# A batched matmul bound by its transfers: stores of two pairs in one transfer, another engine leading the critical section, another one waiting at the end

## The chip, the core and the metric

The kernel runs on one core of a Trainium2 chip. A core has a matrix engine (TensorE, PE in the profile; its weight loads are PEld), VectorE (DVE), ScalarE (ACT), GpSimd (POOL) and SyncE (SP), and 16 transfer engines (DMA) that move data between the chip's main memory (HBM) and the on-chip SBUF. Transfers are issued from queues: here GpSimd's (a software queue, the only one used here that converts float32 to bfloat16 on the way) and SP's (a hardware queue). Each transfer is spread over all 16 transfer engines, and each engine works through a queue in order. A transfer is complete when all 16 have added 1 to its semaphore, 16 in all.

The metric is the device time of one execution in microseconds (us). Before the change it was 513.2 us, the median of three runs (512.89 to 513.69).

## The reference

```python
def setup_inputs():
    batch, m, k, n = 32, 512, 1024, 768
    return {
        "x": np.random.randn(batch, m, k).astype(np.float32),
        "weight": np.random.randn(batch, k, n).astype(np.float32),
    }

def reference(x, weight):
    return np.matmul(x, weight).astype(np.float32)
```

There are 32 independent products of a 512 x 1024 with a 1024 x 768 matrix. All inputs and outputs are float32 in HBM: 67 MB of x, 101 MB of weights, 50 MB of output.

## The kernel before

All of it is written out by hand, with hand-made semaphores, inside one critical section of the Tile framework (L374). That section has a leading engine, SP by default: at its start SP sets a semaphore on which the other engines wait, and at its end SP announces that it is done, every engine drains and answers, and SP collects the answers. A barrier over all engines, led by GpSimd, follows (L407). Lines of waits and transfers below are those of the profile.

**Tiling.** Weights of a batch are loaded as bfloat16 into one of four slots (`w`); batches 4 to 27 are loaded two at a time in one transfer (`load_w`, L100; the others at L104). x is loaded in pairs of batches, 2k+1 and 2k+2, into two slots (`load_x`, L117); batch 0 comes alone through SP (L375), batch 31 at L115. TensorE transposes x through PSUM (`transpose`, L169, eight groups for a pair of batches), VectorE spreads the transposed blocks into `both`, and TensorE multiplies (`multiply`, L150, four groups of 128 rows for a batch). The results of a group of rows leave PSUM through ScalarE (L281, L284) and VectorE (L295, L297).

**Outputs.** The results of two batches, 2a and 2a+1, fill one of four output slots, `outs[a % 4]`: rows of the first batch lie on 64 partitions, those of the second on the other 64, so that every partition holds 24 KB that are contiguous in HBM. `store` (L125) sends such a pair, 3 MB, in one transfer. Before ScalarE and VectorE write into a slot again, `slot_free` waits for the store of the pair four before. The last two batches, 30 and 31 (pair 15), go out as four half-batch stores of 768 KB from SP (`store_half`, L131), batch 30 from a slot of its own, `one`.

**Order of the work.** Each engine's program is a list in the order of the batches.
- GpSimd (`on_pool`) issues nearly all transfers. In the turn of an odd batch b it loads x of pair (b+3)/2, once that slot's transposes are done, then stores pair a = (b-5)/2, then loads the weights of batches b+3 and b+4, once batch b is multiplied. Pairs 0 to 10 are stored so. In the turn of batch 28, the last with loads behind it, it stores pairs 11, 12 and 13, one after the other.
- SP (`on_sp`) passes the arrival of weights on to TensorE, then issues the half of batch 30, pair 14 (3 MB), the second half of batch 30, and the halves of batch 31; all five count on `s_fin`, up to 80. It then sets `s_zero` and waits for `s_fin` (L363).
- TensorE (`pair_on_pe`) takes x, transposes a pair of batches, waits for weights (`take`, L173) and multiplies the two batches.
- GpSimd's last work, `clear_on_pool`, waits for its own stores (`s_st`) and for `s_zero`, then resets and clears all semaphores but `s_fin`.

Of the kernel before, what the change touches and what calls it, by code (L numbers as in the profile page):

```python
# [7 lines left out]
F32 = mybir.dt.float32  # L8
# [4 lines left out]
def kernel(  # L13
# [7 lines left out]
    B, M, K = x.shape  # L21
    _, _, N = weight.shape
    P = 128
    H = P // 2
    MT = M // P
# [3 lines left out]
    ROW = MT * N  # L29
    AHEAD = 3  # L30
    LATE = 4
    HELD = 4
    GROUPS = 2 * MT
    W_SLOTS, X_SLOTS, OUT_SLOTS = 4, 2, 4
# [3 lines left out]
    pe, dve, act, pool, sp = nc.tensor, nc.vector, nc.scalar, nc.gpsimd, nc.sync  # L38
# [3 lines left out]
    x_view = x.rearrange("b (mi mo) k -> b mi mo k", mi=P)  # L42
    pair_view = x[1:B - 1].rearrange("(p r) (mi mo) k -> p (r mi) mo k", r=2, mo=2 * MT)
    out_view = out.rearrange("b (mi mo) n -> b mi (mo n)", mi=P)
    two_view = out.rearrange("(p r) (i m) n -> p (r i) (m n)", r=2, m=2 * MT)

    def sbuf(name, shape, dtype):
        return nc.alloc_sbuf_tensor(name, shape, dtype).ap()
# [3 lines left out]
    ws = [all_ws[:, i] for i in range(W_SLOTS)]  # L52
    xs = [sbuf(f"x{i}", [P, 2 * MT, K], BF16) for i in range(X_SLOTS)]
    both = [sbuf(f"xT{i}", [P, 2, JT, 2, H, 2], BF16) for i in range(MT)]
    outs = [sbuf(f"out{i}", [P, 2 * ROW], F32) for i in range(OUT_SLOTS)]
    one = sbuf("one", [P, ROW], F32)
    x_first = outs[3][:, :MT * K].rearrange("p (mo k) -> p mo k", mo=MT)
    pts = [nc.alloc_psum_tensor(f"pt{i}", [P, JT, P], F32).ap() for i in range(2)]
# [6 lines left out]
    def sem(name):  # L65
        sems.append(nc.alloc_semaphore(name))
        return sems[-1]
# [7 lines left out]
    s_st = [sem(f"s_st{i}") for i in range(OUT_SLOTS)]  # L75
    s_fin = sem("s_fin")
# [9 lines left out]
    def out_done(b):  # L86
        return 2 * (b + 1)
# [4 lines left out]
    def together(b):  # L92
        return W_SLOTS <= b < B - W_SLOTS

    def load_w(b):
        if together(b):
            if b % 2 == 0:
                pool.wait_ge(s_mm, mm_done(b + 1 - W_SLOTS))
                slots = all_ws[:, b % W_SLOTS:b % W_SLOTS + 2].rearrange("p r ko n -> p r (ko n)")
                pool.dma_start(out=slots, in_=w_two_view[b // 2]).then_inc(s_w[b % W_SLOTS], 16)  # L100
            return
        if b >= W_SLOTS:
            pool.wait_ge(s_mm, mm_done(b - W_SLOTS))
        pool.dma_start(out=ws[b % W_SLOTS], in_=w_view[b]).then_inc(s_w[b % W_SLOTS], 16)  # L104

    def loads_of_w(b):

        return sum(not (together(i) and i % 2) for i in range(b % W_SLOTS, b + 1, W_SLOTS))

    def load_x(k):  # L110
        if k >= X_SLOTS:
            pool.wait_ge(s_pt, pt_done(k - X_SLOTS))
        slot = xs[k % X_SLOTS]
        if 2 * k + 1 == B - 1:
            pool.dma_start(out=slot[:, :MT], in_=x_view[B - 1]).then_inc(s_x[k % X_SLOTS], 16)  # L115
        else:
            pool.dma_start(out=slot, in_=pair_view[k]).then_inc(s_x[k % X_SLOTS], 16)  # L117

    def copied(eng, j):
        eng.wait_ge(s_ap, j + 1)  # L120
        eng.wait_ge(s_dp, j + 1)

    def store(eng, a, sem):
        copied(eng, out_done(2 * a + 1) - 1)
        eng.dma_start(out=two_view[a], in_=outs[a % OUT_SLOTS]).then_inc(sem, 16)  # L125

    def store_half(b, p):
        src = one if b == B - 2 else outs[(b // 2) % OUT_SLOTS]
        half = slice(p * N2, (p + 1) * N2)
        copied(sp, 2 * b + p)  # L130
        sp.dma_start(out=out_view[b, :, half], in_=src[:, half]).then_inc(s_fin, 16)  # L131
# [64 lines left out]
    def on_pe():  # L196
        pe.wait_ge(s_ident, 1)
        pe.wait_ge(s_first, 16)
        for g in range(GROUPS):
            if g > 1:  # L200
                pe.wait_ge(s_c, g - 1)
            transpose(0, g)
        pe.wait_ge(s_c, GROUPS).then_inc(s_c, -GROUPS)
        take(s_wr)
        for mt in range(MT):
            multiply(0, mt)
        with pe.Fori(0, LOOPS):
            for q in range(2):
                pair_on_pe(q, q)
            pe.wait_ge(s_c, 2 * GROUPS).then_inc(s_c, -2 * GROUPS)  # L210
            pe.wait_ge(s_a, 9).then_inc(s_a, -8)
            pe.wait_ge(s_d, 9).then_inc(s_d, -8)
        pair_on_pe(LOOPED, 0)
        b = B - 1
        take(s_xr)
        for g in range(MT):
            pe.wait_ge(s_c, GROUPS + max(g - 1, 0))
            transpose(b, g)
        take(s_wr)
        for mt in range(MT):  # L220
            j = 2 * b + mt // 2
            pe.wait_ge(s_c, GROUPS + mt + 1)
            pe.wait_ge(s_ap if mt % 2 else s_a, j - 1 if mt % 2 else 5 + mt // 2)
            pe.wait_ge(s_dp, j - 1)
            multiply(b, mt)
# [30 lines left out]

    def slot_free(eng, b):
        a = b // 2
        if a >= OUT_SLOTS and b % 2 == 0 and b < B - 2:
            eng.wait_ge(s_st[a % OUT_SLOTS], 16 * (a // OUT_SLOTS))  # L260
        if b == B - 1:
            eng.wait_ge(s_st[a % OUT_SLOTS], 16 * (a // OUT_SLOTS))

    def pieces(b, p, i):

# [9 lines left out]
    def out_on_act(b, p):  # L275
        j = 2 * b + p
        if p == 0:
            slot_free(act, b)
        act.wait_ge(s_mm, 2 * j + 1)
        for piece in pieces(b, p, 0):  # L280
            last = act.copy(*piece)  # L281
        last.then_inc(s_a, 1)
        act.wait_ge(s_mm, 2 * j + 2)
        act.copy(*pieces(b, p, 2)[0]).then_inc(s_ap, 1)  # L284
# [38 lines left out]

    def on_pool():
        load_w(0)
        pool.memset(ident, 0.0).then_inc(s_zero, 1)
        pool.wait_ge(s_zero, 1)
        pool.affine_select(
            out=ident,
            in_=ident,  # L330
            compare_op=mybir.AluOpType.not_equal,
            fill=1.0,
            base=0,
            pattern=[[-1, P]],
            channel_multiplier=1,
        ).then_inc(s_ident, 1)
        load_x(0)
        load_w(1)
        load_w(2)
        load_x(1)  # L340
        for b in range(B):
            if b % 2 and b + AHEAD + 1 < B:
                load_x((b + AHEAD) // 2)
            a = (b - 5) // 2
            if b % 2 and 0 <= a < B // 2 - 1 - HELD:
                store(pool, a, s_st[a % OUT_SLOTS])
            if b + AHEAD < B:
                load_w(b + AHEAD)
            if b == B - LATE:
                for a in range(B // 2 - 1 - HELD, B // 2 - 2):  # L350
                    store(pool, a, s_st[a % OUT_SLOTS])

    def on_sp():
        for b in range(B):
            if not (together(b) and b % 2):
                landed(sp, s_w[b % W_SLOTS], loads_of_w(b), s_wr, 1 + together(b))
        store_half(B - 2, 0)
        store(sp, B // 2 - 2, s_fin)
        store_half(B - 2, 1)
        store_half(B - 1, 0)  # L360
        store_half(B - 1, 1)
        sp.sem_inc(s_zero, 1)
        sp.wait_ge(s_fin, 80).then_inc(s_fin, -80)  # L363

    def clear_on_pool():

        for i, s in enumerate(s_st):
            pool.wait_ge(s, 16 * len(range(i, B // 2 - 2, OUT_SLOTS)))
        pool.wait_ge(s_zero, 2)
        used = range(sems[0].num, s_fin.num)  # L370
        pool.dma_reset(used)
        pool.sem_clear(used)

    with tc.tile_critical():  # L374
        sp.dma_start(x_first, x_view[0]).then_inc(s_first, 16)  # L375
        on_pool()
        on_pe()
        on_dve()
        on_act()
        on_sp()  # L380
        clear_on_pool()
# [30 lines left out]
```

## Time and profile before

| | |
|---|---|
| median of three runs | 513.2 us (512.89 to 513.69) |
| profiled execution, device time | 513.58 us |
| its span, first to last instruction | 511.8 us |
| mean granted TensorE clock | 0.946 |
| TensorE busy | 434.8 us (85%) |
| VectorE, ScalarE, GpSimd busy | 40%, 22%, 6% |
| transfers on GpSimd's queue | 14 stores of 3 MB, 12 weight loads of two batches, 8 of one, 16 loads of x |
| read and written in HBM | 167.77 MB and 50.33 MB, 426 GB/s over the span |

The profile is one execution. Its busy times don't add up to the span, since engines work side by side; the row of the transfer engines gives, for each of 40 slices of the span, the mean share of time in which they were busy, in tenths. The "GB/s" beside it counts bytes at the SBUF end: loads that turn float32 into bfloat16 count half of what they read. TensorE's clock is granted in steps: the profile lists stretches at full and at half clock.

### The profile page before, as it was taken

The numbers are of one execution on the slowest core, as the hardware profiler recorded it, in microseconds if no ns is written. First come the engines' busy times: TensorE is split into PE (matmuls) and PEld (weight loads), VectorE is DVE, ScalarE is ACT, GpSimd is POOL, SyncE is SP. The second block draws the span as 40 slices with busy tenths as digits, with TensorE's granted clock in tenths as the row PEclk, the third lists the DMA queues.
The fourth block names the chain that finished last, engine by engine and source line by source line (L and its number), as shares of the span: only waits on it lengthen the run. The fifth ranks groups of instructions, "written<-read, shape, count | busy, mean of one in ns | idle before, by whom it ended". The sixth has DMA issues, their size and how long they took to land. (4 is left out here: it accounts for less than half of the span.)

```text
span 511.8 us, 6037 instructions
## 1 busy us (share of the span) xinstructions
PE 434.8 (85%) x2528; PEld 278.5 (54%) x2576; DVE 207.0 (40%) x332; ACT 110.2 (22%) x189; POOL 29.8 (6%) x56
## 2 busy tenths in 40 slices
PE   0899975999998698987979989699897988999993
PEld 0666642666565364653646546365463644666561
DVE  0463540545445063451533525235252451545330
ACT  1013120132222112221212221122211222132210
POOL 3000000000101000010000100001000010010000
PEclk9999995999999799997989989799898997999998
DMA  8999999999999999999999999999999999999997
GB/s 255 212 216 218 224 208 224 208 230 327 220 331 220 242 312 223 332 221 254 297 224 335 219 267 283 217 340 215 277 273 220 335 219 298 256 217 249 428 428 309
DMA packets 9611, 135.40 MB, mean 265 GB/s; under 512 B 896, under 2 KB 896, under 8 KB 1408
## 3 DMA queue, kind: packets, MB, share of 16 engines
q0 software_dynamic: 8736, 126.88, 96.4%
q1 hardware_dynamic: 864, 8.39, 4.0%
q8 instruction: 5, 0.08, 0.1%
q14 instruction: 6, 0.05, 0.0%
HBM read 167.77 MB, written 50.33 MB: 426 GB/s over the span
## 5 line engine op out<-in xcount | busy, mean ns | idle before, releaser
L150 PE MATMUL pm<-w,xT 128*128 128x256 bf16 (+1 forms) x2000 | 351.0, 336 | 44.9 <-PEq L173 42.4
L150 PEld LDWEIGHTS pm<-w,xT 128*128 128x128 bf16 x2048 | 205.7, 101 | 188.1 <-issue 63.2
L295 DVE COPY out<-pm 64x512 f32<-64x512 f32 x120 | 82.5, 687 | 200.7 <-PE pm L150 199.9
L281 ACT COPY out<-pm 64x512 f32<-64x512 f32 (+1 forms) x122 | 70.7, 580 | 294.7 <-PE pm L150 294.0
L249 DVE COPY xT<-pt 128x1024 bf16<-128x1024 bf16 x112 | 72.2, 687 | 61.0 <-PE pt L169 61.0
L169 PE MATMUL pt<-ident,x 128*128 128x128 f32 x496 | 79.9, 302 | 10.5 <-DVE xT L249 9.5
L169 PEld LDWEIGHTS pt<-ident,x 128*128 128x128 f32 x496 | 69.2, 209 | 21.8 <-DVE xT L249 17.5
L284 ACT COPY out<-pm 64x512 f32<-64x512 f32 (+1 forms) x62 | 35.8, 578 | 89.7 <-PE pm L150 89.7
L297 DVE COPY out<-pm 64x512 f32<-64x512 f32 x60 | 41.2, 686 | 0.0
L117 POOL DMA_DIRECT2D x<-in_x_dram x15 | 8.3, 555 | 271.1 <-PE pt L169 270.9
L169 PE MATMUL pt<-ident,out 128*128 128x128 f32 x32 | 6.7, 360 | 12.7 <-DMA out<-in_x_dram 12.3
L100 POOL DMA_DIRECT2D w<-in_weight_dram x12 | 8.4, 703 | 112.8 <-PE pm L150 112.8
L169 PEld LDWEIGHTS pt<-ident,out 128*128 128x128 f32 x32 | 5.1, 206 | 14.1 <-issue 12.3
L232 DVE CAST xT<-pt 128x256 bf16<-128x256 f32 x16 | 6.2, 440 | 14.0 <-PE pt L169 13.8
L125 POOL DMA_DIRECT2D out_dram<-out x14 | 7.5, 537 | 0.7 <-DVE out L297 0.7
L104 POOL DMA_DIRECT2D w<-in_weight_dram x8 | 4.4, 556 | 19.2 <-PE pm L150 18.1
L247 DVE COPY xT<-pt 128x512 bf16<-128x512 bf16 x8 | 3.4, 420 | 4.1 <-PE pt L169 4.1
L292 DVE COPY out<-pm 128x512 f32<-128x512 f32 x2 | 1.4, 692 | 8.4 <-PE pm L150 8.4
L252 DVE COPY xT<-pt 128x1024 bf16<-128x1024 bf16 x4 | 2.6, 686 | 5.2 <-PE pt L169 5.2
L248 DVE COPY xT<-pt 128x512 bf16<-128x512 bf16 x8 | 3.3, 415 | 0.0
L292 DVE COPY one<-pm 128x512 f32<-128x512 f32 x2 | 1.4, 686 | 3.2 <-PE pm L150 3.2
L281 ACT COPY one<-pm 128x512 f32<-128x512 f32 x2 | 1.2, 585 | 4.0 <-PE pm L150 4.0
(9 smaller groups left out, 3.9 us busy)
## 6 DMA issues: line engine op xcount, KB each, us to landing
out_dram<-out POOLq DMA_DIRECT2D x14, 3072.0 KB, 29.7
w<-in_weight_dram POOLq DMA_DIRECT2D x12, 3072.0 KB, 34.1
x<-in_x_dram POOLq DMA_DIRECT2D x15, 2048.0 KB, 23.0
w<-in_weight_dram POOLq DMA_DIRECT2D x8, 1536.0 KB, 32.2
out_dram<-out SPq DMA_DIRECT2D x1, 3072.0 KB, 18.5
out<-in_x_dram SPq DMA_DIRECT2D x1, 2048.0 KB, 11.3
out_dram<-one SPq DMA_DIRECT2D x2, 768.0 KB, 12.4
out_dram<-out SPq DMA_DIRECT2D x2, 768.0 KB, 8.2
```

What stands on the lines that cost most here:

```text
L100: pool.dma_start(out=slots, in_=w_two_view[b // 2]).then_inc(s_w[b % W_SLOTS], 16)
L104: pool.dma_start(out=ws[b % W_SLOTS], in_=w_view[b]).then_inc(s_w[b % W_SLOTS], 16)
L117: pool.dma_start(out=slot, in_=pair_view[k]).then_inc(s_x[k % X_SLOTS], 16)
L125: eng.dma_start(out=two_view[a], in_=outs[a % OUT_SLOTS]).then_inc(sem, 16)
L150: last = pe.matmul(pm[bank][:, at:at + size], xT[:, ko // 2, :, ko % 2], w[:, ko, off:off + size], start=(ko == 0), stop=(ko == KT - 1),)
L169: last = pe.transpose(pts[g % 2][:, i, :], rows, ident)
L232: last = dve.tensor_copy(xT[:, 2 * (g % 2) + j].rearrange("p (h i) r -> p r h i", h=2), pt[:, 2 * j:2 * j + 2].rearrange("p r (i h) -> p r ...
L249: return dve.tensor_copy(tile[:, :, :, half].rearrange("p b j i r -> p j b i r"), pt)
L281: last = act.copy(*piece)
L284: act.copy(*pieces(b, p, 2)[0]).then_inc(s_ap, 1)
L295: last = dve.tensor_copy(*piece)
L297: dve.tensor_copy(*pieces(b, p, 2)[1]).then_inc(s_dp, 1)
```

## The change

It has three parts. First, the output slots become one tensor, so that two neighbouring slots can be sent in one transfer: GpSimd now stores pairs (0,1), (2,3), (4,5), (6,7) and (8,9) together, four batches and 6 MB each, in the turns of batches 5, 9, 13, 17 and 21, where pairs 0, 2, 4, 6 and 8 went; the turns of 7, 11, 15, 19 and 23 have no store. Pair 10 goes alone in the turn of batch 25, and in the turn of batch 28 pair 11 goes alone and pairs 12 and 13 together. A double store counts on the semaphore of its first slot, and `await_store` finds the count that a given pair's store brings. Second, the critical section is led by ScalarE, and its end leaves out GpSimd's drain. Third, GpSimd and not SP waits for the five last stores.

```diff
+    four_view = out.rearrange("(q s r) (i m) n -> q (r i) s (m n)", s=2, r=2, m=2 * MT)
...
-    outs = [sbuf(f"out{i}", [P, 2 * ROW], F32) for i in range(OUT_SLOTS)]
+    all_outs = sbuf("out", [P, OUT_SLOTS, 2 * ROW], F32)
+    outs = [all_outs[:, i] for i in range(OUT_SLOTS)]
...
-    def store(eng, a, sem):
-        copied(eng, out_done(2 * a + 1) - 1)
-        eng.dma_start(out=two_view[a], in_=outs[a % OUT_SLOTS]).then_inc(sem, 16)
+    STORES = [(a, 2) for a in range(0, B // 2 - 1 - HELD - 1, 2)]
+    STORES += [(B // 2 - 2 - HELD, 1), (B // 2 - 1 - HELD, 1), (B // 2 - HELD, 2)]
+
+    def store(eng, a, n, sem):
+        copied(eng, out_done(2 * (a + n - 1) + 1) - 1)
+        at = a % OUT_SLOTS
+        to, of = (four_view[a // 2], all_outs[:, at:at + 2]) if n == 2 else (two_view[a], outs[at])
+        eng.dma_start(out=to, in_=of).then_inc(sem, 16)
+
+    def store_on_pool(i):
+        a, n = STORES[i]
+        store(pool, a, n, s_st[a % OUT_SLOTS])
+
+    def await_store(eng, a):
+        first = next(i for i, n in STORES if i <= a < i + n)
+        done = sum(i % OUT_SLOTS == first % OUT_SLOTS for i, _ in STORES if i <= first)
+        eng.wait_ge(s_st[first % OUT_SLOTS], 16 * done)
...
     def slot_free(eng, b):
         a = b // 2
-        if a >= OUT_SLOTS and b % 2 == 0 and b < B - 2:
-            eng.wait_ge(s_st[a % OUT_SLOTS], 16 * (a // OUT_SLOTS))
-        if b == B - 1:
-            eng.wait_ge(s_st[a % OUT_SLOTS], 16 * (a // OUT_SLOTS))
+        if b == B - 1 or (a >= OUT_SLOTS and b % 2 == 0 and b < B - 2):
+            await_store(eng, a - OUT_SLOTS)
...
             a = (b - 5) // 2
-            if b % 2 and 0 <= a < B // 2 - 1 - HELD:
-                store(pool, a, s_st[a % OUT_SLOTS])
+            for i, (first, _) in enumerate(STORES[:-2]):
+                if b % 2 and a == first:
+                    store_on_pool(i)
...
             if b == B - LATE:
-                for a in range(B // 2 - 1 - HELD, B // 2 - 2):
-                    store(pool, a, s_st[a % OUT_SLOTS])
+                store_on_pool(-2)
+                store_on_pool(-1)
...
         sp.sem_inc(s_zero, 1)
-        sp.wait_ge(s_fin, 80).then_inc(s_fin, -80)
...
         pool.dma_reset(used)
         pool.sem_clear(used)
-
-    with tc.tile_critical():
+        pool.wait_ge(s_fin, 80).then_inc(s_fin, -80)
+
+    with tc.tile_critical(sync_engine=mybir.EngineType.Activation, no_gpsimd_drain=True):
```

More of the change, by code (lines that the diff above doesn't have):

```diff
@@ L357, in on_sp @@
         store_half(B - 2, 0)
-        store(sp, B // 2 - 2, s_fin)
+        store(sp, B // 2 - 2, 1, s_fin)
         store_half(B - 2, 1)
@@ L362, in on_sp @@
         sp.sem_inc(s_zero, 1)
-        sp.wait_ge(s_fin, 80).then_inc(s_fin, -80)
     def clear_on_pool():
         for i, s in enumerate(s_st):
-            pool.wait_ge(s, 16 * len(range(i, B // 2 - 2, OUT_SLOTS)))
+            done = sum(a % OUT_SLOTS == i for a, _ in STORES)
+            if done:
+                pool.wait_ge(s, 16 * done)
         pool.wait_ge(s_zero, 2)
```

## The prediction

> **What bounds the kernel now.** I read the page's summary first, then stretches of the end, then the two queues that issue transfers, and TensorE's waits last. From the page:
>
> ```profile
> PE 434.8 (85%) x2528; PEld 278.5 (54%) x2576; DVE 207.0 (40%) x332; ACT 110.2 (22%) x189; POOL 29.8 (6%) x56
> ...
> DMA  8999999999999999999999999999999999999997
> ...
> HBM read 167.77 MB, written 50.33 MB: 426 GB/s over the span
> ...
> PE 14%; DVE 1%; issue 0%
> ```
>
> The DMA row is 9 in all slices but the first and the last, while the chain of work covers only 15% of the span: what came before its start is a wait for a load. The 218.1 MB at 426 GB/s are the span: 16 transfer engines, never idle, set the time. TensorE (85% with its cold stretches) has some 5 us to spare for every two batches. So an edit counts for what it does to the transfer engines' first byte, to their work, to whether they run dry, and to what follows their last byte. The end, by stretches (us, PE, PEld, DVE, ACT and POOL busy, clock, DMA share, GB/s):
>
> ```profile
> 400.00:500.00 100.00, 93.59 (x558) 60.50 (x566) 42.95 (x74) 22.63 (x39) 5.33 (x10) 0.97 1.01 306
> ...
> 506.00:508.00 2.00, 0.00 (x0) 0.00 (x0) 0.00 (x0) 0.00 (x0) 0.00 (x0) 0.87 0.96 399
> 508.00:509.00 1.00, 0.00 (x0) 0.00 (x0) 0.00 (x0) 0.00 (x0) 0.00 (x0) 0.50 0.44 184
> 509.00:510.00 1.00, 0.00 (x0) 0.00 (x0) 0.00 (x0) 0.00 (x0) 0.00 (x0) 0.50 0.21 86
> 510.00:511.00 1.00, 0.00 (x0) 0.00 (x0) 0.00 (x0) 0.00 (x0) 0.00 (x0) 0.50 0.02 6
> ```
>
> The 16 engines don't end together. From 508 on a share of 0.44, then 0.21, works on: in the record of landings the first engine ends the last store at 508.20 and the last one at 510.64, 2.4 us later. That slowest engine is the kernel's bound, and it has work waiting to the end. The queues of SP and POOL (start, us, what):
>
> ```profile
> 503.72 0.33 SPq L131 DMA_DIRECT2D out_dram<-out  x1
> ...
> 347.99 0.54 POOL L125 DMA_DIRECT2D out_dram<-out  x1
> 357.83 0.70 POOL L100 DMA_DIRECT2D w<-in_weight_dram  x1 [9.31 <-PE pm L150]
> 378.37 0.56 POOL L117 DMA_DIRECT2D x<-in_x_dram  x1 [19.84 <-PE pt L169]
> 378.93 0.54 POOL L125 DMA_DIRECT2D out_dram<-out  x1
> 388.77 0.70 POOL L100 DMA_DIRECT2D w<-in_weight_dram  x1 [9.31 <-PE pm L150]
> 409.91 0.56 POOL L117 DMA_DIRECT2D x<-in_x_dram  x1 [20.43 <-PE pt L169]
> ```
>
> POOL issues in threes (x, store, weights of two batches), each set some 10 to 13 us before the weights already queued have landed (391.67 and 423.16 for those issued at 357.83 and 388.77). The last store goes out at 503.72. TensorE near the end:
>
> ```profile
> 392.00 11.95 PE L150 MATMUL pm<-w,xT 128*128 128x512 bf16 x63 [3.52 <-PEq L173]
> ...
> 409.66 10.35 PE L150 MATMUL pm<-w,xT 128*128 128x256 bf16 x62
> 423.48 0.80 PE L150 MATMUL pm<-w,xT 128*128 128x512 bf16 x2 [3.48 <-PEq L173]
> ```
>
> Each even batch waits for its weights (L173), and from batch 26 at 423.48 TensorE never waits for a load again: its end, 502.9, follows from that start.
>
> **1. Five pairs of stores become five transfers.** Before, pairs 0 to 9 leave POOL one at a time, ten transfers; after, five of 6 MB (with pairs 12 and 13 as a sixth), so 14 become 8. A double store goes out where its first pair did, so one set in two carries two stores and the next none. GpSimd waits no longer there: the same turn (batch 5, say) first waits for the transposes of batches 5 and 6, to load x, and the copies of batch 3, the last that the double store needs, were over before batch 4 was multiplied, more than 10 us earlier. The copies that use a slot again (slot_free) wait for a store that stands, in the same queue, ahead of the weights of their own batch, so that wait never ends last.
>
> What six transfers less save: the bytes are the same. Landings in unbroken queue traffic: a weight load of one batch 7.25 us (440.18 to 447.43 to 454.68), one of two batches 14.48 us (median of ten): two singles cost 0.02 us more than one double. That is the same edit on the other side. Upper bound: two stores of 7.30 us (mean of 11) against a double load of the same HBM bytes, 0.10 us. Lower bound: writes that alternate between places 3 MB apart could go slower; the paired weight load alternates over the same distance at no loss, so I allow 0.05 us for each of six the wrong way. Six times: -0.12 us near the paired load; I take -0.15, ends -0.6 and +0.3. (Title "DMA: Bandwidth & Descriptors", Anatomy of one DMA: the Trainium skill gives each transfer a fixed cost of about 2 us, mostly the receipt of its last write. By that, an estimate of 6 x 2 = 12 us would go, 501 us. The landings above, with 0.02 us, say that in a full queue it is hidden.)
>
> **2. Weights behind a double store land 7.3 us later, every second time.** TensorE then waits about 7.2 us for batches 8, 12, 16, 20 and 24 (before: 3.5 at 24) and little for 10 to 26. Two things hang on it.
>
> Does the queue run dry? At batch 20, say, weights land at 328.2 + 7.3 = 335.5, TensorE starts 0.3 later, the batch takes 13.2 (10.35, and 2.9 of cold clock as at 423.48), transposes 5.8: POOL issues x and the double store at 354.8. The weights queued by then land at 357.1 on the fastest engine and 359.9 on the slowest: 2.3 and 5.1 us left, against 3.6 and 5.0 at the smallest such place of before (x at 101.48, landings 105.1 to 106.4), which shows no gap. A fast engine that idles costs nothing until it has lost its 2.4 us lead. I take 0.
>
> Does TensorE's end move the last store? Weights of batch 24 at 391.67 + 7.3 = 399.0; start 399.3; batch 12.0 to 13.3 (rows 392.00 and 423.48, the latter 13.25 long), transposes 5.9, batch 25 10.4: batch 26 can start at 427.4 to 428.8, not at 423.5. Its weights, with the same bytes queued ahead of them as before, are there at 423.2, so it has no wait, and without one no cold start (-2.9). TensorE is then 1.0 to 2.4 us later to the end, and the last store goes out at up to 506.1. For the slowest engine that is enough: eight packets of 6144 B take it 1.9 us, it starts them at 508.4, and the store needs 1.0 us from issue to first byte (SP's first load: 0.95 to 1.96), so there are 508.4 - 504.7 = 3.7 us of slack. Cost 0; ends 0 and, see the rival, +1.5. (Title "TensorE: Matmul & The Clock Gate", Part 1: the Trainium skill says that an idle window of about 3.4 us puts the clock to half until one busy window has passed, so a wait twice as long costs no second penalty. The waits of 3.5 us here cost 1.6 and 2.9; by the page at most half of two windows, 3.4, an estimate, and batch 26 would start 0.5 us later than I have it, still within the slack.)
>
> **3. ScalarE leads the critical section.** At the start SP issues its event at 0.73 and its own first load at 0.95, behind it; that event (0.07 to its branch at 0.80, against 0.76 for ScalarE) moves to ScalarE, whose table load has 11 us of cover. SP's load comes 0.03 us sooner; GpSimd's path is as long. ScalarE's one event late in its copies has no reader waiting. -0.03, ends 0 and -0.07.
>
> **4. The end.** SP's last wait now:
>
> ```profile
> L363 SPq EVENT_SEMAPHORE  x1: 17/17/17, 510.7 to 510.7; - x1
> ...
> L374 SPq EVENT_SEMAPHORE  x3: 17/28/28, 510.7 to 510.9; - x3
> L374 SPq NOP  x2: 13/13/13, 0.7 to 511.0; - x2
> ...
> L407 POOLq EVENT_SEMAPHORE  x4: 17/17/17, 511.2 to 511.7; - x4
> ```
>
> From the last landing (510.64): SP wakes 510.66, tells all 510.72, engines drain 510.76 to 510.81, SP collects 510.88 and 510.95, event 511.02, drains to 511.13, GpSimd's first barrier 511.16, end 511.77. After: every engine but GpSimd has answered when TensorE ends; GpSimd wakes at 510.66, an event (about 0.08 between its own, 511.16 to 511.24), SP and ScalarE wake and drain (0.12), barrier at about 510.90. One trip out and back becomes one out: -0.25, ends 0 and -0.4. GpSimd's drain (0.05) ran beside the others'. Behind its new wait (on the five final stores) only the barrier is queued; its clearing of semaphores ran at 504.2 in both.
>
> Sum: -0.15 - 0.03 - 0.25 = -0.43 us. On the profiled execution: span 511.8 to 511.4, time 513.58 (span and 1.8 around it) to 513.15. That execution is 0.4 above the median of the runs, 513.2, from which I get **512.8 us**. A measurement here tells about 0.2%, 1.0 us: this is within it.
>
> **Rivals.**
> - *The last store comes too late (slower).* Batch 24 and batch 26 both run cold: then TensorE is 5.3 us late (7.3 - 3.5 + 1.5), 1.6 beyond the slack of 3.7, and with -0.43 the time is 514.4. For: every wait over 2.6 us in the trace brought half clock. Against: batch 26 has no wait left. It decides from 3.7 us of lateness; over 0.2% from 5.2. The same price falls due if the slowest engine waits for POOL in three of the five long turns by 0.5 us. Chance 0.10.
> - *More is saved (faster).* The six transfers save 0.10 each, the barrier 0.4, and the slowest engine loses 0.2 or more of its 2.4 us lag, which grew over the run (0.7 us at 25 us, 2.8 at 390): 513.2 - 0.6 - 0.4 - 0.2 = 512.0. For: lag is the slow engines' alone, and nothing says that it doesn't come with transfers. Against: it jumps at instruction fetches (0.8 at 30 us), which stay. Chance 0.22.
> - *The merge does nothing.* Transfers save 0, the end 0.25: 512.9, in the same class as the forecast.
>
> **How the numbers follow.** Forecast with the third rival 0.68, slower 0.10 (0.12 with what I don't see), faster 0.20. The likeliest case alone runs from 512.2 to 513.5 (sum of the ends and the 0.4 between runs). For 8 in 10 I go to the faster case, 511.9, and most of the way to the slower, 514.0.
>
> **What would show it.** Eight out_dram transfers on POOL's queue instead of 14, six of them of 6 MB; DMA at 9 throughout; waits at L173 alternating between about 7 and under 1 us; last matmul 1 to 2.4 us later, at 504 to 505.3, with the last landing unchanged at about 510.4; from there to the end 0.85 us instead of 1.1. I am wrong if the DMA share falls below 1 in mid-run, if all 16 engines end together after the last store's issue, or if the double stores take much else than 14.5 us to land.

## The result: slower by 0.27%, and where the time went

The changed kernel takes 514.35 us in the median of 14 executions (513.11 to 519.03), the kernel before 513.36 us (512.89 to 513.93) beside it on the same chip. The two medians are 0.99 us apart. The ratio on record is 1.0027, with an interval of 1.0014 to 1.0040, which leaves no change out; the time lies outside the predicted range of 511.9 to 514.0. The spread has changed too: the fastest five executions lie at 513.1 to 513.5, among those of before, while five of the 14 take 515 us or more, which the kernel before never did.

The profiled execution of the changed kernel took 514.30 us (span 512.5), that of before 513.58 (span 511.8). From the page of the changed kernel, its summary:

```profile
DMA  8999999999999999999999999999999999999997
...
HBM read 167.77 MB, written 50.33 MB: 426 GB/s over the span
...
L167 PE MATMUL pm<-w,xT 128*128 128x256 bf16 (+1 forms) x2048 | 349.6, 334 | 50.2 <-PEq L190 50.2
...
out_dram<-out POOLq DMA_DIRECT2D x6, 6144.0 KB, 29.5
```

The row of the transfer engines is as full as before: nothing here says that they ran dry. The waits for weights, L173 before and L190 now, have grown to 50.2 us: one of 1.1 us at the start and six of 7.4 to 8.6 us, in place of twelve of 42.4 us together. The six transfers of 6 MB are there.

The end, by stretches as before (us, PE, PEld, DVE, ACT and POOL busy, clock, DMA share, GB/s):

```profile
506.00:508.00 2.00, 0.00 (x0) 0.00 (x0) 0.00 (x0) 0.00 (x0) 0.00 (x0) 1.00 1.02 427
508.00:509.00 1.00, 0.00 (x0) 0.00 (x0) 0.00 (x0) 0.00 (x0) 0.00 (x0) 1.00 0.89 369
509.00:510.00 1.00, 0.00 (x0) 0.00 (x0) 0.00 (x0) 0.00 (x0) 0.00 (x0) 0.96 0.43 180
510.00:511.00 1.00, 0.00 (x0) 0.00 (x0) 0.00 (x0) 0.00 (x0) 0.00 (x0) 0.50 0.16 68
```

Compared with before, the decline begins one microsecond later: a share of 0.43 at 509 where it was 0.44 at 508. In the record of landings the first engine ends the last store at 509.14 (before 508.20) and the last one at 511.61 (before 510.64). The distance between them is the same, 2.47 and 2.44 us. So the first and the last engine are late by nearly the same, 0.94 and 0.97 us. They did not wait for the last store: it was issued at 505.77, and the share is still 1.02 from 506 to 508.

The time before that end holds the loss. Each packet of a kind has a usual duration in the trace; a packet of x, which writes 16 KB, takes 1.227 us. Summed over all packets that take over 0.05 us more than usual, the excess, divided by 16 engines, is 1.66 us before and 2.62 us after: 0.95 us more, which is the later end. The largest lot, 0.99 us, is in one load of x, the one that GpSimd issues at 291.44, in front of the double store of pairs 8 and 9. GpSimd's queue there, in the changed kernel (start, us, what):

```profile
291.44 0.57 POOL L119 DMA_DIRECT2D x<-in_x_dram  x1 [26.36 <-PE pt L186]
292.00 0.71 POOL L133 DMA_DIRECT2D out_dram<-out  x1
301.84 0.71 POOL L102 DMA_DIRECT2D w<-in_weight_dram  x1 [9.12 <-PE pm L167]
```

The weights queued ahead of that load landed at 294.14 on the first engine and 296.03 on the last. The first packet of x ran at 293.85, 2.41 us after its issue. The stretches over that load of x, which ends at about 306:

```profile
294.00:301.00 7.00, 7.00 (x45) 4.21 (x43) 1.98 (x3) 2.67 (x5) 0.00 (x0) 1.00 1.00 212
301.00:304.00 3.00, 3.00 (x20) 1.78 (x19) 1.98 (x3) 0.58 (x1) 0.71 (x1) 1.00 1.08 164
304.00:308.00 4.00, 4.00 (x27) 2.42 (x25) 1.14 (x2) 1.74 (x3) 0.00 (x0) 1.00 0.90 367
```

In the kernel before, the same load was issued at 283.34, and its first packet ran at nearly the same time, 293.75. The same stretches there:

```profile
294.00:301.00 7.00, 4.35 (x20) 2.34 (x21) 1.47 (x3) 0.28 (x2) 0.44 (x1) 0.76 1.03 220
301.00:304.00 3.00, 3.00 (x21) 1.73 (x19) 0.61 (x1) 1.52 (x3) 0.00 (x0) 1.00 1.03 257
304.00:308.00 4.00, 3.95 (x26) 2.44 (x26) 1.37 (x3) 1.16 (x2) 0.00 (x0) 1.00 0.97 408
```

In the changed kernel the share in the last column but one stays near 1, but the bytes in the last column fall from 212 to 164 GB/s from 301 to 304. The engines are busy with packets of x that take up to 2.1 us. This is a loss that the row of tenths cannot show. It sits in the last third of the load, some nine to thirteen microseconds after it was issued.

### The profile page after: what moved, and what is told of

Its sections match the earlier page's. It is cut to its first block, busy times and chain, and to the rows that moved or that the text cites. A ratio compares the mean times of both kernels' runs of the same rounds, so it can differ in the third digit from the quotient of the medians.

```text
span 512.5 us, 6075 instructions
## 1 busy us (share of the span) xinstructions
PE 431.7 (84%) x2576; PEld 277.6 (54%) x2576; DVE 206.9 (40%) x332; ACT 110.3 (22%) x189; POOL 27.7 (5%) x50
## 5 line engine op out<-in xcount | busy, mean ns | idle before, releaser
L167 PE MATMUL pm<-w,xT 128*128 128x256 bf16 (+1 forms) x2048 | 349.6, 334 | 50.2 <-PEq L190 50.2
L133 POOL DMA_DIRECT2D out_dram<-out x8 | 5.3, 668 | 1.3 <-DVE out L312 1.3
```

The source lines that it names most:

```text
L133: eng.dma_start(out=to, in_=of).then_inc(sem, 16)
L167: last = pe.matmul(pm[bank][:, at:at + size], xT[:, ko // 2, :, ko % 2], w[:, ko, off:off + size], start=(ko == 0), stop=(ko == KT - 1),)
```

## The experiments

I call the time from the issue of a load of x to its first packet its *lead*: how much work the queue still held. Loads are named by the pair they bring: x4 is issued in the turn of batch 5, x5 in that of batch 7, x6 in that of batch 9, and so on up to x14 in that of batch 25. In the changed kernel the even ones go out in the turns of a double store (x14 in that of a single one), with only the weights ahead of them.

The theories: first, that the double store itself costs time, by its shape; second, that the later order does, in that the queue is short when x and the store are issued; third, that the cost comes from addresses, when the rows of x and the bytes around them lie an even 32 KB apart; fourth, that the end is at fault. Later ones are told where they came up.

### The merge alone

Part one of the change, with SP leading and waiting as before:

```diff
         sp.sem_inc(s_zero, 1)
+        sp.wait_ge(s_fin, 80).then_inc(s_fin, -80)
...
-        pool.wait_ge(s_fin, 80).then_inc(s_fin, -80)
...
-    with tc.tile_critical(sync_engine=mybir.EngineType.Activation, no_gpsimd_drain=True):
+    with tc.tile_critical():
```

> The double stores alone, with SP leading and waiting as before. In the profile of the changed kernel every us lost against before lies in a few stretches in which the packets of an x load (16 KB written, 1.23 us each) take 1.4 to 2.1 us on all 16 engines: 0.96 us at 301 to 304, 0.28 at 428 to 430. Theory A (the double stores bring more such stretches): median 514.3 to 514.9, runs spread over 2 us or more, as with the whole change, plus the 0.27 us that the end's part saved. Rival B (the part with ScalarE and GpSimd at the ends makes the loss): 513.0 to 513.5, runs within 1 us.

Measured: 513.65 us (513.31 to 519.88, 12 runs) against 513.27, the median of the kernel before, run beside it; ratio 1.0033 (1.0007 to 1.0058). Four of the 12 are at 515 or above. The median lies between the two ranges that I had named, but the spread is that of theory A: the slowing and the scatter come with the merge.

### The ends alone

Parts two and three on the kernel before:

```diff
-        sp.wait_ge(s_fin, 80).then_inc(s_fin, -80)
...
+        pool.wait_ge(s_fin, 80).then_inc(s_fin, -80)
...
-    with tc.tile_critical():
+    with tc.tile_critical(sync_engine=mybir.EngineType.Activation, no_gpsimd_drain=True):
```

> ScalarE leading and GpSimd waiting alone, with single stores as before. Theory A: the last landing as before and 0.85 us instead of 1.13 from there to the end, so 0.3 us less than before, about 513.1, runs within 1 us. Rival B: 514 or more, runs spread over 2 us.

Measured: 513.18 us (512.63 to 514.13, 11 runs) against 513.27; ratio 0.9998 (0.9990 to 1.0007), no execution above 514.2. The ends cost nothing; what they save is too little for this measurement, and is read from the profiles below.

### Two single stores in the place of a double one

The kernel before, with two stores of 3 MB, one right behind the other, where the double store would go:

```diff
-            if b % 2 and 0 <= a < B // 2 - 1 - HELD:
-                store(pool, a, s_st[a % OUT_SLOTS])
+            if b % 2 and 0 <= a < B // 2 - 1 - HELD and a % 2 == 0:
+                for i in range(a, min(a + 2, B // 2 - 1 - HELD)):
+                    store(pool, i, s_st[i % OUT_SLOTS])
```

> As before, but two single stores go out in the turns in which the change sends a double one, and none in the turns between: the bytes stand in the queue in the order of the change, in 14 transfers instead of 8. Theory A1 (the order, or what it does to the time at which x loads and GpSimd's issues meet, is to blame): 514.3 to 515, spread over 2 us or more, weights of every second pair 7.3 us late. Rival A2 (the shape of the 6 MB transfer, two places 3 MB apart written in turn, is to blame): 513.2 to 513.6, within 1 us.

Measured: 513.72 us (513.42 to 519.31, 12 runs); ratio 1.0026 (1.0004 to 1.0047), with two executions at 518 and 519. Again the median falls between the two ranges and the spread decides: the slowing and the scatter come without any transfer of 6 MB: it is where the bytes stand in the queue, not the shape of the transfer. The first theory falls.

### Other addresses for x

The changed kernel, with the pair loads of x reading from the weights, 36 KB apart from partition to partition and not 32:

```diff
+    PITCH = 2 * MT * K + K
...
-            pool.dma_start(out=slot, in_=pair_view[k]).then_inc(s_x[k % X_SLOTS], 16)
+            pool.dma_start(out=slot, in_=pair_at(k)).then_inc(s_x[k % X_SLOTS], 16)
```

> The whole change, but the pair loads of x read other data: 32 KB for each partition as before, but out of the weights and 36 KB apart instead of 32 KB, so the products of batches 1 to 30 are of wrong numbers; sizes, order and counts of all transfers are the same. Theory C (the slow stretches come from x rows 32 KB apart, a power of two, when engines come to read in step): no x packet over 1.3 us, 512.4 to 512.8, runs within 1 us. Rival (the stretches have to do with the order of traffic or with GpSimd's issues, whatever the addresses): 514.3, spread over 2 us.

Measured: 513.30 us (513.13 to 514.71, 11 runs); ratio 1.0004 (0.9995 to 1.0013), in neither of the two ranges. The scatter was gone but for one execution, which spoke for addresses. But the leads of its profiled execution were 2.81 to 4.16 us, longer than those of the changed kernel (2.38 to 3.57), so that the two theories had not been told apart. The tenth run below does so.

### The double store ahead of x

The changed kernel, with the store issued in front of the load of x in each turn:

```diff
         for b in range(B):
-            if b % 2 and b + AHEAD + 1 < B:
-                load_x((b + AHEAD) // 2)
             a = (b - 5) // 2
...
+            if b % 2 and b + AHEAD + 1 < B:
+                load_x((b + AHEAD) // 2)
```

> The whole change, with the double store issued ahead of the x load in its turn instead of behind it. It waits only for copies that are done some 20 us before TensorE has finished the transposes that the x load waits for, so 14.5 us of stores lie in the queue when x is issued. Theory D (the late weights make GpSimd issue x 2.4 to 3.5 us before the first engine needs it, and in executions where TensorE is a little colder the queue runs dry): no execution over 514, median 512.4 to 512.8, issue of x to its first packet over 12 us everywhere. Rival O (two stores in a row, in whatever place, disturb the transfers): 513.5 to 514.5, with executions of 515 to 519 in 2 to 5 of 12.

Measured: 513.27 us (513.09 to 513.55, 11 runs) against 513.14; ratio 1.0002 (0.9993 to 1.0011). Of the load of x nothing is lost any more: every x has 7 us or more queued ahead of it, and no packet of x took longer than usual. The scatter is gone. But this is not the 512.4 to 512.8 that I had expected: the loss went, and a gain over before did not appear. In this order the store of pairs 8 and 9 does not wait for the transposes, so it goes out 24.9 us ahead of x:

```profile
266.37 0.72 POOL L133 DMA_DIRECT2D out_dram<-out  x1 [1.63 <-DVE out L312]
291.27 0.54 POOL L119 DMA_DIRECT2D x<-in_x_dram  x1 [24.19 <-PE pt L186]
```

It runs from 294 to 301 at full rate, but it was not issued at a short queue, so this run doesn't tell what a store would lose there:

```profile
294.00:301.00 7.00, 7.00 (x46) 4.22 (x44) 1.99 (x3) 2.50 (x5) 0.00 (x0) 1.00 1.01 427
```

### x made late without any change of stores

The kernel before, with GpSimd waiting for three of the four groups of the batch before it issues x and the store, from the turn of batch 9 on:

```diff
             if b % 2 and b + AHEAD + 1 < B:
+                if b >= 9:
+                    pool.wait_ge(s_mm, 4 * b + 3)
                 load_x((b + AHEAD) // 2)
```

> Before, with single stores in their old order, but from the turn of batch 9 on GpSimd also waits for three of the four groups of that turn's batch before it issues x and the store, 7.8 us later than now: from issue of x to its first packet 2 to 5 us instead of 9 to 13. Theory D: executions of 515 or more in several of 12, median 514 or more. Rival O (the order of the stores): like before, 513.2 to 513.4, within 1 us.

Measured: 521.77 us (519.77 to 522.50, 5 runs) against 513.14; ratio 1.0156 (1.0141 to 1.0172). In its profiled execution the leads of x alternate between 3.1 to 5.4 us and 1.25 to 1.48 us. Each of the first kind loses 0.08 us or less, each of the four short ones 1.80 to 2.08 us. All slow packets of that execution make 8.7 us, against 1.7 before; its span was 8.9 us longer than that of before (520.7 against 511.8). The rest is idle time at the short places, 0.7 us in the mean of the engines, and engines that end further apart. Single stores, doubles left out, ends as before: a short queue is enough for the loss. From the queue and the stretches of this run:

```profile
294.65 0.56 POOL L117 DMA_DIRECT2D x<-in_x_dram  x1 [31.22 <-PE pm L150]
```

```profile
301.00:304.00 3.00, 3.00 (x13) 1.50 (x12) 0.00 (x0) 0.08 (x1) 0.00 (x0) 0.56 1.08 208
304.00:308.00 4.00, 4.00 (x26) 2.44 (x25) 1.45 (x3) 1.66 (x3) 0.00 (x0) 1.00 0.94 160
```

x was issued three microseconds later than in the changed kernel, and the dip to 160 GB/s comes some three microseconds later too, at 304 to 308, again about ten microseconds after the issue.

### A shorter multiplication

The changed kernel, with six of the eight K parts multiplied, so that TensorE is done sooner and x is issued sooner:

```diff
-        for ko in range(KT):
+        for ko in range(KT - 2):
...
-                    stop=(ko == KT - 1),
+                    stop=(ko == KT - 3),
```

> The whole change, with the products over 6 of the 8 parts of K only (the last two left out of every batch). All transfers and their order are unchanged; TensorE needs about 2.6 us less for a batch, so GpSimd issues x and the double store 2.6 us earlier after the late weights: 5 to 6 us to the first packet instead of 2.4 to 3.5. Theory D: no execution over 514, median 512.4 to 512.9. Rival O: as the whole change, 514.3, spread to 519.

Measured: 512.70 us (512.48 to 513.12, 11 runs) against 513.14; ratio 0.9992 (0.9983 to 1.0001), an interval that just takes in no change. With double stores, x in front of them and the new ends all in place, and the lead longer (5.0 to 6.4 us at the double turns), the loss is gone. The lead is not all that differs: TensorE also does less, and the last store goes out at 487.91 and not at 505.77. The load issued at 291.44 in the changed kernel goes out at 287.75, and its stretches stay up:

```profile
287.75 0.57 POOL L119 DMA_DIRECT2D x<-in_x_dram  x1 [31.63 <-PE pt L186]
```

```profile
301.00:304.00 3.00, 3.00 (x20) 1.84 (x19) 1.69 (x3) 1.38 (x3) 0.00 (x0) 1.00 1.03 268
304.00:308.00 4.00, 3.51 (x24) 3.01 (x23) 2.58 (x4) 0.58 (x1) 0.00 (x0) 1.00 0.98 414
```

### Single stores ahead of x

The kernel before with the new ends, and each single store in front of its load of x:

```diff
         for b in range(B):
-            if b % 2 and b + AHEAD + 1 < B:
-                load_x((b + AHEAD) // 2)
...
+            if b % 2 and b + AHEAD + 1 < B:
+                load_x((b + AHEAD) // 2)
             if b + AHEAD < B:
...
```

> Before, with ScalarE leading and GpSimd waiting at the end as in the change, single stores in their turns, but each store issued ahead of the x load. Theory D: as the ends alone (513.18, 512.63 to 514.13 measured), the queue never short, and nothing more to gain: 512.8 to 513.2. Rival O2 (the small losses in x packets, some 0.4 us in every profile so far, come where a store follows an x load in the queue): 512.4 to 512.7, no x packet over 1.3 us beyond the first.

Measured: 515.45 us (514.85 to 515.77, 5 runs); ratio 1.0043 (1.0029 to 1.0057). Neither expectation foresaw this. It is another loss: no load of x is slow here (0.01 us at most), all slow packets together make 1.8 us, about what they make before (1.7). But a few engines fall behind the others. Of the weights that land around 330, twelve engines have brought theirs by 326.33 and the other four at 327.36, 329.21, 329.40 and 329.94. The landings of one transfer spread over 4.4 us there and 5.4 us at 440, against 2.6 to 2.8 before, and the last store ends at 512.76 on the slowest engine, 3.7 us after the median one. Around the end of the weights ahead of most stores, three to six packets took 0.1 to 0.9 us longer than usual. Why some engines pay for that order was not found.

### Doubles to pair 7, singles behind them

To take the better order where it helps and leave the end of the program as before: pairs 0 to 7 as double stores ahead of x, pairs 8 and 9 as singles behind it.

```diff
-    STORES = [(a, 2) for a in range(0, B // 2 - 1 - HELD - 1, 2)]
+    STORES = [(a, 2) for a in range(0, 8, 2)] + [(8, 1), (9, 1)]
...
+            a = (b - 5) // 2
+            for i, (first, n) in enumerate(STORES[:-2]):
+                if b % 2 and a == first and n == 2:
+                    store_on_pool(i)
             if b % 2 and b + AHEAD + 1 < B:
                 load_x((b + AHEAD) // 2)
...
+                if b % 2 and a == first and n == 1:
```

> A version that takes what the runs so far point to: double stores for pairs 0 to 7 only, each ahead of its x load; pairs 8, 9 and 10 singly, behind their x loads, as before; the ends as in the change. Queue never short (12 us or more from issue of x to its first packet in the double turns, 9 or more in the others), and TensorE's last wait for weights at batch 26 again, so its end at 503 and not at 504 to 505. Theory D: 512.7 to 513.0, no execution over 514, so a little under before. If the stores of the double turns cost by themselves: 513.3 or more.

Measured: 513.58 us (513.04 to 515.71, 12 runs); ratio 1.0008 (0.9997 to 1.0019). Three of the 12 stand above 514. In its profiled execution (514.61 us) all loads of x but one lose nothing; x12, at the border between the two orders, is issued at 354.83 with a lead of 1.89 us and loses 1.66 us. I had overlooked that border: the last double store leaves TensorE late by one turn more, and there x stood first again.

### Late x from other addresses

The late x of the sixth run, with the addresses of the fourth (both edits as above, on the kernel before).

> The kernel with the late x issue (521.8 us), with the pair loads of x reading weights 36 KB apart instead of x rows 32 KB apart, so the products of batches 1 to 30 are of wrong numbers. Theory D: the loss comes from the short queue alone, 520 to 523. Rival C (the addresses of x are what makes a short queue costly): 514 or less.

Measured: 520.94 us (520.56 and 521.32); ratio 1.0150 (1.0132 to 1.0168). Loads with leads of 1.30 to 1.48 us lose 1.50 to 2.01 us, as they did from x itself. The theory of addresses falls; the fourth run was fast for its leads.

### Two more executions of the changed kernel

The changed kernel itself, unedited, twice, to see the lead in executions of different length.

> The changed kernel again, for the profile of one of its slow executions (five of 14 were at 515 or more). Theory D: in an execution of 515 or more, one or more of the even x loads 6 to 14 has a first packet less than 2.3 us after its issue and loses 1 to 2 us over its packets; in one under 513.6 none does.

> As the look before: one more execution of the changed kernel. Theory D: its time stands above 512.7 by what the even x loads with short queues lose in it, within 0.5 us.

Measured: 520.55 and 514.62 us. The long one shows, at the same places as in the first profile, leads of 2.08, 1.29, 1.31 and 1.28 us at x8, x10, x12 and x14, and losses of 1.23, 1.70, 1.83 and 1.65, together 6.4 us; its span is 7.0 us longer than that of the kernel before. So the expectation for a long execution held. From its queue and stretches:

```profile
293.50 0.57 POOL L119 DMA_DIRECT2D x<-in_x_dram  x1 [27.26 <-PE pt L186]
```

```profile
294.00:301.00 7.00, 7.00 (x46) 4.26 (x45) 3.81 (x6) 1.74 (x3) 0.77 (x2) 1.00 1.01 204
301.00:304.00 3.00, 2.95 (x20) 1.73 (x19) 0.36 (x1) 1.52 (x3) 0.10 (x1) 1.00 1.03 197
304.00:308.00 4.00, 4.00 (x27) 2.44 (x26) 1.62 (x3) 1.38 (x3) 0.61 (x1) 1.00 0.93 213
```

At 304 to 308 the store should be running at 367 GB/s or more, and x is still at 213. The short one of the two has one lead below 2.8 us, 2.31 at x14, and loses 0.83 there. Its expectation failed: all its even loads lose 1.0 us, which gives 513.7 and not 514.62. Here one engine ended the last store at 511.93, 1.5 us after all others (510.46; in the first profile 511.61 after 511.45). So not every long time of the changed kernel is loss in x, and why that engine was late is open.

All loads of x with their first packet after 100 us and a lead under 6.5 us, in the profiled executions of all kernels here, before and after among them (us; a loss is the mean over 16 engines of what its packets took beyond the usual):

| lead from issue to first packet | loads | loss in each |
|---|---|---|
| 1.25 to 1.48 | 10 of a full pair of batches | 1.50 to 2.08 |
| 1.29 | 1 of a single batch | 0.31 |
| 1.89 and 2.08 | 2 | 1.66, 1.23 |
| 2.31 to 2.91 | 10 | 0.00 to 0.99, median 0.23 |
| 3.01 to 6.38 | 44 | 0.00 to 0.15 |

Not one lead is shorter than 1.25 us. Whether the queue still holds 3 us or 10 makes no difference (of the loads above 6.5 us, one lost 0.39 us and the others 0.10 at most); from 3 us down to 2 the loss grows to more than a microsecond. It is not the idle time of a queue that ran empty, which at leads of 2.4 us did not happen (at 1.3 us it comes on top, with 0.1 to 0.2 us). It is in packets that take longer: at the leads of 2.08 us and less, 0.1 to 0.6 us in the first half of the load and 1.1 to 1.7 in the second.

One rival to the lead alone is not tested. Each of the 22 loads of a full pair with a lead under 3 us had a store right behind it in the queue. With the store there and a lead of 3 us or more the loss was 0.15 us or less but for one load with 0.39, so the store alone is not the cause; whether a short lead without a store behind it would cost the same, no run shows. The one load that had weights behind it (1.29 us, a single batch) lost its 0.31 us in its first packets, and it was over 9 us after its issue.

Much of the scatter follows from this, in a way that I read from two executions and didn't test by an edit. A loss of 1 us delays all that stands behind it, the next long wait of TensorE ends later, the batch after the wait starts later by so much (at 404.38 in the long execution, 399.50 in the profiled one), and the next x is issued nearer to the end of its queue. A lead once below 2.1 us stays there: 2.08, 1.29, 1.31, 1.28.

### Is the rest the order at the border, or the late end?

The ninth run with its border mended: pair 8, too, is stored ahead of x.

```diff
-                if b % 2 and a == first and n == 2:
+                if b % 2 and a == first and (n == 2 or a == 8):
...
-                if b % 2 and a == first and n == 1:
+                if b % 2 and a == first and n == 1 and a != 8:
```

> The version with double stores of pairs 0 to 7 ahead of their x loads, mended where its queue fell short: pair 8, stored singly, also goes ahead of its x load; pairs 9 and 10 go behind theirs. Waits from issue of x to its first packet are then 8 us or more everywhere, so no execution over 514 by theory D. If what the store-first version (513.27) still misses of 512.7 is TensorE's late end, this one, whose weights for batch 26 come when they come before, stands at 512.7 to 512.9. If it is the slowest transfer engine, which falls back by 0.35 us where a double store follows weights, it stays at 513.1 to 513.4.

Measured: 513.09 us (512.80 to 513.54, 11 runs) against 513.08; ratio 0.9998 (0.9989 to 1.0007). With the border mended, no load of x from x4 on loses more than 0.05 us and the scatter is gone, but there is no gain.

And the fifth run with the last three batches (29 to 31) multiplied over six of eight K parts, so that TensorE ends sooner than before (the last store goes out at 497.10, before at 503.72):

```diff
-        for ko in range(KT):
+        parts = KT - 2 if b > B - 4 else KT
+        for ko in range(parts):
...
-                    stop=(ko == KT - 1),
+                    stop=(ko == parts - 1),
```

> The store-first version (513.27), with the products of batches 29, 30 and 31 over 6 of the 8 parts of K only, so TensorE ends about 7.5 us sooner and the last stores are issued well before the engines are free; all else is the same. Late end: 512.7 to 512.9. Slowest transfer engine: 513.1 to 513.3.

Measured: 513.10 us (512.87 to 513.44, 11 runs) against 513.08; ratio 0.9999 (0.9990 to 1.0008). The fifth run stood 0.13 above its own kernel before and this one 0.02, so that a late end can have cost the fifth some 0.1 us, less than either interval tells. What else keeps the fifth, the thirteenth and this one from the 0.4 us that the shorter multiplication shows was not settled. In their profiled executions the slowest engine is further behind, by 2.7 to 3.4 us in the median of the landings between 440 and 476 us, against 2.3 in the shorter multiplication and 2.4 with the ends alone; but it was 2.8 in the kernel before too, and 2.0 in the fourth run with its 513.30 us. Three executions of the changed kernel had 2.7, 2.7 and 3.5, so this is no account.

No version that does all of the work was faster than the kernel before by more than the measurement tells: the only one with a median lower by 0.4 us leaves a quarter of the multiplication out.

## Why the prediction was wrong, step by step

**The step that failed is in part 2, "Does the queue run dry?", with its price "I take 0".** Its working was near enough: I had 2.3 us left on the fastest engine at a long turn, counted to the landing of the weights ahead, and by that count the profiled execution had 2.70, 2.73 and 3.07 at three of them and 3.63 and 3.65 at two. (As leads, which end some 0.3 us sooner, these are 2.41, 2.38, 2.73, 3.29 and 3.34.) What failed is the price. I reasoned that a queue with 2.3 us left is not dry, that only a fast engine would idle, and that it had a lead of 2.4 us over the slowest one to lose. The runs show another loss: with less than about 3 us queued, packets of the load of x take longer, the slowest engine's among them (the load issued at 291.44 landed at 304.74 on the first and 307.14 on the last engine, the same load before at 303.79 and 306.35). In the profiled execution the three short leads cost 0.99, 0.39 and 0.22 us. In other executions leads of 2.1 us and below, about what my 2.3 us comes to as a lead, cost 1.2 to 2.1 us per full load.

I had compared with one place of before, "x at 101.48", that showed no gap. By its lead of 3.31 us (3.6 in my reckoning) it lies just on the harmless side. The row nearest to 2.3 was not near enough, and I did not bound the price from the other side, as I did for the transfers. The rival of the slower side named the right turns ("the slowest engine waits for POOL in three of the five long turns") but took the loss for idle time of 0.5 us, and gave it no chance of its own.

It also made my own sign useless. "I am wrong if the DMA share falls below 1 in mid-run" can't show packets that are busy for longer: the share was 1.08 while the bytes fell to 164 GB/s. The column of GB/s beside it, over a few microseconds, would have been the sign.

**Part 1, the merge: right as to its price, as far as it can be told.** A double store lands 14.58 and 14.59 us behind the transfer ahead of it (at 194.30 and 130.95), as the two singles did, 2 x 7.30. The Trainium skill's fixed cost of about 2 us for each transfer (title "DMA: Bandwidth & Descriptors", Anatomy of one DMA) would have given 12 us for six transfers, an estimate; no run here gained more than 0.44 us, so in a full queue it is hidden, as the landings of before said. With the lead made longer (the shorter multiplication), merge and ends together gave -0.44 us beside a forecast sum of -0.43. That kernel also leaves work out, and its interval takes in no change, so the agreement is no proof of the single terms. A slip that moves nothing: my upper bound of 0.10 us for one pair is 0.12 by its own rows (2 x 7.30 less 14.48).

**Part 2, TensorE's end: right.** Long waits alternate with none; batch 24 waited 8.53 us, took 12.81, and batches 25 and 26 ran on without a wait. From the record of TensorE:

```profile
399.50 12.81 PE L167 MATMUL pm<-w,xT 128*128 128x512 bf16 x64 [8.53 <-PEq L190]
...
417.81 20.96 PE L167 MATMUL pm<-w,xT 128*128 128x512 bf16 x128
```

Batch 24's weights landed at 399.17, 7.5 us later than before (forecast 7.3), those of batch 26 at 423.39 (before 423.16), and batch 26 started at about 428.3, half way through the 20.96 us (forecast 427.4 to 428.8). TensorE ended at 504.96, 2.05 us later (forecast 1.0 to 2.4), the last store went out at 505.77 (forecast up to 506.1), and the engines still ended 2.47 us apart. So the last store is not the cause, and the rival that had it so is wrong. A wait of 8.53 us brought a batch of 12.81 us, one of 3.48 us, before the change, 13.24: a longer wait had no second penalty. The Trainium skill's rule, from which I had taken that, agrees here: an idle window of about 3.4 us puts the clock to half until a busy window has passed (title "TensorE: Matmul & The Clock Gate", Part 1).

**Part 3, ScalarE leading: right as to the issue, with no gain that shows.** SP's first load is issued at 0.93 us, 0.95 before; 0.03 was forecast. It landed at 12.28 and not at 12.21, so nothing of this reached TensorE.

**Part 4, the end: right.** From the last landing to the end of the span it takes 0.91 us (511.61 to 512.52), 1.13 before (510.64 to 511.77): -0.22, where I had -0.25 and named 0.85. The changed kernel's last instructions, by line (duration in ns: least, median, largest; then the first and the last start, us):

```profile
L390 POOLq EVENT_SEMAPHORE  x1: 17/17/17, 511.6 to 511.6; - x1
...
L392 ACTq NOP  x2: 14/14/14, 0.7 to 511.8; - x2
L392 POOLq NOP  x1: 13/13/13, 511.7 to 511.7; - x1
```

GpSimd wakes with the landing, and the drains follow within 0.2 us, with no collecting by SP. Its clearing of semaphores ran at 506.9 and not at 504.2 as I had it, still 4.7 us ahead of the last landing.

The sum against the measured: 0.97 us later in the last landing less 0.22 saved behind it is 0.75 us, which is what the two profiled spans differ by (512.52 and 511.77); the device times differ by 0.72. In these two executions all of the sign comes from the term that I put at 0.

## What to carry to other kernels

When an edit moves bytes ahead of a load on which the issuing engine's next turn depends, compute at every turn how much work the queue still holds when the next transfer is issued, and treat a margin that is smaller than any the old trace shows as an unknown price, not as nothing; here 3 us was enough, and 2.1 us or less cost more than 1 us for each load of a full pair. Read bytes per second over a few microseconds and not the busy share alone, since slow packets count as busy. What is ready to go, such as a store, belongs in front of what is issued late; but each order has to be measured, for the same move with single stores cost 2.3 us (515.45 against 513.18 with the ends alone) through a few engines that fell behind.

## What was not expected of the hardware

- A queue that is short when a transfer is issued costs most at the end of that transfer, not at its beginning: 1.1 to 1.7 of 1.2 to 2.1 us fall on the second half of the load, mostly 9 to 13 us after its issue. At leads from 1.25 to 2.41 us alike, 95% of that part comes later than 9.0 to 9.8 us after the issue. Why there is left open, and so is what a store would lose in that place.
- The shortest time from the issue of a load of x on GpSimd's queue to its first packet was 1.25 us, over all runs.
- The 16 engines drift apart over the run: the spread of the landings between 440 and 476 us was 2.0 to 3.5 us in fifteen profiles, three of the changed kernel alone among them with 2.7, 2.7 and 3.5, and 5.4 with single stores ahead of x, where three engines fall far behind and a fourth less. Only the last is clear of what executions of one kernel differ by. The slowest engine sets the end, and in that order this cost 2.3 us; what makes some engines slower was not found.
